# Placing the high and low parts of the activations in sixteen shifted tiles

## The chip, the core and the metric

The kernel runs on one core of a Trainium2 chip. The metric is the device time of one execution in microseconds (us). Three runs of the kernel before took 1261.02, 1261.59 and 1265.77 us; the median is 1261.59 us.

## What is computed

A decoder trunk of two layers on 512 tokens of width 1024, in float32. Cut to what matters here:

```python
for l in range(2):
    h = rmsnorm(x, attn_norm_w[l])
    proj = h @ w_in[l]                      # 22 tiles of 128 columns and one group of 148
    ...                                     # three mixers: state space, short convolution, sparse attention
    x = x + concat(y_ssd, y_sc, y_nsa) @ w_out[l]
    h = rmsnorm(x, ffn_norm_w[l])
    u = causal_dwconv(h @ ffn_w_up[l], ffn_conv_w[l], ffn_conv_b[l])   # 43 tiles of 128 columns
    gate, val = split(u)
    x = x + (silu(gate) * val) @ ffn_w_down[l]
return rmsnorm(x, final_norm_w)
```

## The kernel before

The activations lie transposed: eight tiles `x[k]` of 128 features by 512 tokens. A matmul that needs more precision than one float32r pass is made of three: each operand is split in a high part (rounded to float32r) and a low part (what the rounding left), and `mul3` (lines 185 to 190) multiplies weight high by activation high (L188), weight high by activation low (L189) and weight low by activation high (L190), all into one PSUM tile. The weights are the stationary operand, the activations are the moving one, 512 columns each time.

The activations of both norms are kept in `hs` (L90): eight tiles of 128 x 2 x 512, where `[:, 0, :]` is the high part and `[:, 1, :]` the low part, 2,048 bytes behind it in the same partition. `Norm.split` (L217 to 220) fills them: ScalarE writes the high part (L219), VectorE the low part (L220), 8 + 8 instructions for each of four norms. They are read

- by the 22 input-projection tiles of each layer (`tile_steps`, L430) and by the 43 up-projection tiles (`mtile`, L196), through `mul3`: 65 tiles x 8 values of k x 2 layers = 1,040 triples, 3,120 of the kernel's 5,843 matmuls;
- by `group_steps` (L450, L451), where a 128 x 128 piece of the activations is the stationary operand and the weights (148 columns, high and low) are the moving one: 64 matmuls with the high part and 64 with the low part. The weights' piece starts `(k % 4) * 148` elements into its tile.

All weights come in chunks of 128 x 1024 by DMA into `raw`; ScalarE and VectorE (or GpSimd) split them into `hl` (L163 to 166), three chunks ahead of their use. Products that are not of `hs` read their activations from `s` tiles (2,048 bytes each, a ring of 32) or from `yS`. `small` (L77) gives tiles of 256 bytes for columns and small matrices, from a ring of 21.

The order on every engine is that of the program: in the mixers one step of the projection stream (`pull`) is laid between pieces of the attention and of the state-space scan by a table of weights (`PLAN`); the feed-forward part is a plain sequence of tiles.

In the built program the tiles lie one behind the other in each partition, each start rounded up to a multiple of 32 bytes. `h0` starts at byte 32,928, that is 32 bytes behind a multiple of 64. As all that follows has sizes that are multiples of 64, every `h`, `hl`, `s` and `yS` tile starts 32 bytes behind a multiple of 64; `h` tiles start at 160 modulo 2,048, the other three at 672.

Of the kernel before, what the change touches and what calls it, by code (L numbers as in the profile page):

```python
# [10 lines left out]
F32 = mybir.dt.float32  # L11
F32R = mybir.dt.float32r
AF = mybir.ActivationFunctionType
OP = mybir.AluOpType
AX = mybir.AxisListType

P = 128
D = 1024
T = 512
NL = 2  # L20
KD = 8
# [4 lines left out]
NB = 148  # L26
# [37 lines left out]
def trunk(ctx: ExitStack, tc: tile.TileContext, ins, out):  # L64
    nc = tc.nc
    V, A, G, TE = nc.vector, nc.scalar, nc.gpsimd, nc.tensor

    per = ctx.enter_context(tc.tile_pool(name="per", bufs=1))
    pw = ctx.enter_context(tc.tile_pool(name="pw", bufs=3))
    ph = ctx.enter_context(tc.tile_pool(name="ph", bufs=1))  # L70
# [4 lines left out]
        return ph.tile(list(shape), dt, tag="s", bufs=32, name="s")  # L75

    def small(n, dt=F32):  # L77
        return ph.tile([P, 64], dt, tag="m", bufs=21, name="m")[:, :n]

    def mm():  # L80
        return pp.tile([P, 512], F32, tag="mm", bufs=3, name="mm")

    def aux():
        return pp.tile([P, 512], F32, tag="aux", bufs=4, name="aux")


    x = [per.tile([P, T], F32, name=f"x{k}") for k in range(KD)]
    mhalf = per.tile([P, 4], F32, name="mhalf")
    V.memset(mhalf, -0.5)
    hs = [per.tile([P, 2, T], F32R, name=f"h{k}") for k in range(KD)]  # L90
    par = [per.tile([P, NPAR], F32, name=f"par{l}") for l in range(NL)]
    cst = per.tile([P, K_COS], F32, name="cst")
    rot = per.tile([P, 2 * T], F32, name="rot")
# [75 lines left out]
    def nxt():  # L169
        i = st["use"]  # L170
        st["use"] += 1
        while st["dma"] < min(len(chunks), i + 5):
            do_dma(st["dma"])
            st["dma"] += 1
        while st["prep"] < min(len(chunks), i + 4):
            do_prep(st["prep"])
            st["prep"] += 1
        return hls.pop(i)
# [6 lines left out]
    def mul3(ps, wt, j, rhs_h, rhs_l, first, last):  # L185
        wh = wt[:, 0, j * P:(j + 1) * P]
        wl = wt[:, 1, j * P:(j + 1) * P]
        TE.matmul(ps, wh, rhs_h, start=first, stop=False)  # L188
        TE.matmul(ps, wh, rhs_l, start=False, stop=False)  # L189
        TE.matmul(ps, wl, rhs_h, start=False, stop=last)  # L190

    def mtile():
        wt = nxt()
        ps = mm()
        for k in range(KD):
            mul3(ps, wt, k, hs[k][:, 0, :], hs[k][:, 1, :], k == 0, k == KD - 1)  # L196
        return ps

    def col_rstd(dst, ps, n, width):
        v = small(n)  # L200
        V.tensor_scalar(v, ps, 1.0 / width, EPS, op0=OP.mult, op1=OP.add)  # L201
        G.tensor_tensor(dst, v, mhalf[:, :n], op=OP.pow)  # L202
# [4 lines left out]
    class Norm:  # L207
# [8 lines left out]

        def split(self, k):  # L217
            w = par[self.l][:, self.w + k:self.w + k + 1]
            A.activation(hs[k][:, 0, :], x[k], AF.Copy, scale=w)  # L219
            V.scalar_tensor_tensor(hs[k][:, 1, :], x[k], w, hs[k][:, 0, :].bitcast(F32), op0=OP.mult, op1=OP.subtract)  # L220

        def square(self, k, eng=V):
            sq = slot()
# [6 lines left out]
        def sums(self):  # L230
            ps = pp.tile([P, 512], F32, tag="pv", bufs=1, name="pv")
            acc = self.acc[V]
            if G in self.acc:
                V.tensor_tensor(acc, acc, self.acc[G], op=OP.add)
            for t in range(4):
                TE.matmul(ps[:, t:t + 1], acc[:, t * P:(t + 1) * P], ones[:, 0:1], start=True, stop=True)
            self.col = small(4)
            col_rstd(self.col, ps[:, 0:4], 4, D)
# [12 lines left out]
    def mixers(l, norm):  # L251
# [4 lines left out]
        def evac(ps, n):  # L256

            r, sw = slot(), slot()
            A.activation(r, ps, AF.Copy)
            for q in range(0, n, 64):  # L260
                A.activation(sw[q:q + 32], r[q + 32:q + 64], AF.Copy)
                A.activation(sw[q + 32:q + 64], r[q:q + 32], AF.Copy)
            return r, sw
# [68 lines left out]
        def post_b(t, ps):  # L332
            tmp = ph.tile([P, NB], F32, tag="btmp", bufs=2, name="btmp")
            c1 = cx["col"][:, t:t + 1]
            A.activation(tmp, ps[:, NB:2 * NB], AF.Copy, scale=c1)
            V.scalar_tensor_tensor(bV[:, t * P:(t + 1) * P], ps[:, 0:P], c1, tmp[:, 0:P], op0=OP.mult, op1=OP.add)
            V.scalar_tensor_tensor(bS[:, t, :], ps[:, P:NB], c1, tmp[:, P:NB], op0=OP.mult, op1=OP.add)
# [5 lines left out]
        def values():  # L343
            for b in range(2):
                v3 = Vv[b].rearrange("p (t c) -> p t c", c=P)
                s3 = bV.rearrange("p (t b d) -> p t b d", b=2, d=64)[:, :, b, :]
                A.activation(v3[:, :, 0:64], s3, AF.Copy)
                V.tensor_tensor(v3[:, :, 64:128], s3, v3[:, :, 0:64].bitcast(F32), op=OP.subtract)
            g3 = gate.rearrange("p (t c) -> p t c", c=12)
            A.activation(g3, bS[:, :, 8:20], AF.Tanh, scale=0.5)  # L350
            V.tensor_scalar(gate, gate, 0.5, 0.5, op0=OP.mult, op1=OP.add)
# [61 lines left out]
        def step():  # L413
            clock[0] += 1
            for e_ in [e_ for e_ in timed if e_[0] <= clock[0]]:
                timed.remove(e_)
                e_[1]()
            if clock[0] == t_sums:
                norm.sums()
                cx["col"] = norm.col  # L420
            if clock[0] == t_spread:
                first_norm()
                for p_ in late:
                    p_()

        def tile_steps(name, post, rot_n=0):
            wt = nxt()
            ps = mm()
            for k in range(KD):
                mul3(ps, wt, k, hs[k][:, 0, :], hs[k][:, 1, :], k == 0, k == KD - 1)  # L430
                step()
                if k < KD - 1:
                    yield
            args = evac(ps, rot_n) if rot_n else (ps,)
            if clock[0] < t_spread:
                late.append(lambda: post(*args))
            else:
                post(*args)
            done[name] = True
            yield  # L440

        def group_steps():
            pss = [aux() for _ in range(4)]
            for k in range(KD):
                if k % 4 == 0:
                    wt = nxt()
                w = wt[:, :, (k % 4) * NB:(k % 4 + 1) * NB]
                for t in range(4):
                    tok = slice(t * P, (t + 1) * P)
                    TE.matmul(pss[t][:, 0:2 * NB], hs[k][:, 0, tok], w, start=(k == 0), stop=False)  # L450
                    TE.matmul(pss[t][:, 0:NB], hs[k][:, 1, tok], w[:, 0, :], start=False, stop=(k == KD - 1))  # L451
                if k < KD - 1:
                    step()
                    yield
            late.append(lambda: [post_b(t, pss[t]) for t in range(4)] + [values()])
            step()
            done["group"] = True
            yield
# [59 lines left out]
        def cmp_mlp():  # L518
            pt = aux()
            for kv in range(2):  # L520
                for c in range(2):
                    o_ = TE.matmul(pt[:, kv * 32:kv * 32 + 32], hid[kv][:, c * P:(c + 1) * P], sel, start=(c == 0), stop=(c == 1))
                    if kv == 0 and c == 0:
                        pinned(0, o_)
            h_, t_ = small(64), small(64)
            A.activation(h_, pt[:, 0:64], AF.Copy)
            V.tensor_tensor(t_, h_, h_, op=OP.mult)
            V.tensor_scalar(t_, t_, 0.044715, 1.0, op0=OP.mult, op1=OP.add)
            V.tensor_tensor(t_, t_, h_, op=OP.mult)
            A.activation(t_, t_, AF.Tanh, scale=math.sqrt(2.0 / math.pi))  # L530
            V.scalar_tensor_tensor(h_, t_, 1.0, h_, op0=OP.add, op1=OP.mult)
            state["hid"] = h_
# [332 lines left out]
        for i, it in enumerate(items):  # L865
            t, b, k = it
# [40 lines left out]
        start, acc_w = pulled, 0  # L907
# [11 lines left out]
    def ffn(l, nf):  # L919
# [11 lines left out]
        def pair(i):  # L931
            if i == 0:
                ps = mtile()
                nf.sums()
                pv = mtile()
                nf.spread()
                g, v = up(0, ps), up(1, pv)
                A.activation(g, g, AF.Silu)
            else:
                g = up(2 * i, mtile())  # L940
                A.activation(g, g, AF.Silu)  # L941
                v = up(2 * i + 1, mtile())
            V.tensor_tensor(v, v, g, op=OP.mult)  # L943
            gh, gl = slot(F32R), slot(F32R)
            split(gh, gl, v)
            return gh, gl
# [100 lines left out]
    n = Norm(0, C_ANW)  # L1047
# [7 lines left out]
    for l in range(NL):  # L1055
        n = ffn(l, mixers(l, n))
# [105 lines left out]
```

## Time and profile before

| | us |
|---|---|
| median of 3 runs | 1261.59 |
| the profiled execution, its own time | 1265.31 |
| its span, first to last instruction | 1263.5 |
| TensorE (PE) busy in the span | 1208.4 |
| VectorE (DVE) busy | 879.8 |
| ScalarE (ACT) busy | 580.8 |
| GpSimd (POOL) busy | 221.8 |

The granted TensorE clock over the span was 0.981 of its full 2.4 GHz. The profiled execution took 3.7 us more than the median. A matmul's duration in the profile is from its start to its modelled end and overlaps the next; how long one occupies the engine is read from the distance between starts of neighbours, called pitch here.

### The profile page before, as it was taken

What the parts mean: (1) busy time and instruction counts of PE and PEld (TensorE: products, weight loads), DVE (VectorE), ACT (ScalarE), POOL (GpSimd) and SP (SyncE); (2) the same over time, 40 slices, a digit from 0 to 9 for tenths busy, and PEclk for the clock granted to TensorE, in tenths of its full rate; (3) what the DMA queues carried; (4) which work ended last, traced back from release to release, by engine and by line L of the source; (5) the groups of instructions that cost most, each with busy time, mean ns of one, the idle gap of its engine ahead of it and who ended that gap; (6) DMA issues with size and microseconds to landing.
All of it is one profiled execution on the core that took longest, in us unless ns stands there. A gap on an engine that the chain in (4) does not pass through costs nothing. (4 is left out here: it accounts for less than half of the span.)

```text
span 1263.5 us, 15487 instructions
## 1 busy us (share of the span) xinstructions
PE 1208.4 (96%) x5843; PEld 999.2 (79%) x5843; DVE 879.8 (70%) x1408; ACT 580.8 (46%) x909; POOL 221.8 (18%) x199
## 2 busy tenths in 40 slices
PE   8889899999999999999999888999999999999997
PEld 7667678788888888888877666778888888888897
DVE  6899979567776247776468998794587743677763
ACT  6655554354443124444347455434444422444553
POOL 3442337500000000000043332563000000000001
PEclk9989999999999999999999899999999999999999
DMA  7321123233223332332223211322233323333352
GB/s 259 113 67 51 51 84 101 67 100 98 88 98 100 100 99 90 95 117 87 84 84 100 67 51 51 103 98 83 84 100 101 100 88 96 100 100 100 122 165 99
DMA packets 37051, 121.33 MB, mean 96 GB/s; under 512 B 4144, under 2 KB 6512, under 8 KB 36976
## 3 DMA queue, kind: packets, MB, share of 16 engines
q1 hardware_dynamic: 36832, 120.33, 30.0%
q8 instruction: 46, 0.75, 0.3%
q14 instruction: 29, 0.24, 0.1%
q10 hardware_dynamic: 144, 0.00, 0.0%
HBM read 118.19 MB, written 2.13 MB: 95 GB/s over the span
## 5 line engine op out<-in xcount | busy, mean ns | idle before, releaser
L188 PE MATMUL mm<-h,hl 128*128 128x512 f32 x1040 | 413.6, 398 | 0.8 <-DVE s L359 0.8
L189 PE MATMUL mm<-h,hl 128*128 128x512 f32 x1040 | 410.3, 395 | 0.0
L190 PE MATMUL mm<-h,hl 128*128 128x512 f32 x1040 | 409.7, 394 | 0.0
L165 ACT ACTIVATE hl<-raw 128x1024 fp32r<-128x1024 f32 (+1 forms) x211 | 220.8, 1047 | 236.9 <-PE mm L190 129.5
L166 DVE TENSOR_TENSOR hl<-raw,hl 128x1024 fp32r<-128x1024 f32 (+1 forms) x167 | 203.4, 1219 | 110.3 <-ACT hl L165 108.1
L188 PEld LDWEIGHTS mm<-h,hl 128*128 128x128 f32 x1040 | 197.8, 190 | 42.0 <-issue 1.8
L190 PEld LDWEIGHTS mm<-h,hl 128*128 128x128 f32 x1040 | 197.4, 190 | 41.2 <-issue 0.2
L189 PEld LDWEIGHTS mm<-h,hl 128*128 128x128 f32 x1040 | 197.7, 190 | 39.6 <-issue 0.5
L202 POOL TENSOR_TENSOR m<-m,mhalf 128x1 f32<-128x1 f32 (+2 forms) x14 | 9.9, 709 | 773.7 <-DVE m L201 773.7
L166 POOL TENSOR_TENSOR hl<-raw,hl 128x1024 fp32r<-128x1024 f32 x44 | 108.3, 2464 | 150.5 <-ACT hl L165 144.8
L928 DVE SCALAR_TENSOR_TENSOR s<-s,par 128x511 f32<-128x511 f32 (+1 forms) x172 | 128.3, 748 | 3.5 <-ACT s L926 0.6
L925 DVE TENSOR_TENSOR s<-mm,rstdB 128x512 f32<-128x512 f32 x86 | 59.1, 689 | 66.1 <-PE mm L190 66.1
L189 PE MATMUL mm<-s,hl 128*128 128x512 f32 (+1 forms) x240 | 86.6, 361 | 3.4 <-DVE s L248 3.4
L188 PE MATMUL mm<-s,hl 128*128 128x512 f32 (+1 forms) x240 | 86.5, 360 | 1.1 <-ACT s L247 1.1
L190 PE MATMUL mm<-s,hl 128*128 128x512 f32 (+1 forms) x240 | 86.4, 360 | 0.0
L247 ACT ACTIVATE s<-s 128x512 fp32r<-128x512 f32 (+1 forms) x62 | 33.0, 545 | 111.8 <-DVE s L943 108.0
L188 PE MATMUL aux<-s,hl 128*128 128x512 f32 (+1 forms) x232 | 82.1, 354 | 0.0
L190 PE MATMUL aux<-s,hl 128*128 128x512 f32 (+1 forms) x232 | 81.8, 353 | 0.0
L189 PE MATMUL aux<-s,hl 128*128 128x512 f32 (+1 forms) x232 | 81.8, 353 | 0.0
L926 ACT ACTIVATE s<-s,par 128x512 f32<-128x512 f32 x86 | 69.2, 807 | 8.8 <-DVE s L925 8.1
L248 DVE TENSOR_TENSOR s<-s 128x512 fp32r<-128x512 f32 (+1 forms) x62 | 45.3, 741 | 27.9 <-ACT s L247 27.9
L941 ACT ACTIVATE s<-s 128x512 f32<-128x512 f32 x40 | 25.3, 632 | 79.0 <-DVE s L928 79.0
(252 smaller groups left out, 1648.9 us busy)
## 6 DMA issues: line engine op xcount, KB each, us to landing
raw<-in_w_up SPq DMA_DIRECT2D x86, 512.0 KB, 3.5
raw<-in_w_dn SPq DMA_DIRECT2D x54, 512.0 KB, 3.5
raw<-in_w_in SPq DMA_DIRECT2D x44, 512.0 KB, 3.5
raw<-in_w_out SPq DMA_DIRECT2D x16, 512.0 KB, 3.6
raw<-in_w SPq DMA_DIRECT2D x8, 512.0 KB, 3.6
s<-dr SPq DMA_DIRECT2D x16, 256.0 KB, 4.3
x<-in_xT SPq DMA_DIRECT2D x8, 256.0 KB, 5.8
out<-s SPq DMA_DIRECT2D x8, 256.0 KB, 3.4
```

Of the source, the lines that this page charges most:

```text
L165: A.activation(t[:, 0, a:b], r[:, a:b], AF.Copy)
L166: eng.tensor_tensor(t[:, 1, a:b], r[:, a:b], t[:, 0, a:b].bitcast(F32), op=OP.subtract)
L188: TE.matmul(ps, wh, rhs_h, start=first, stop=False)
L189: TE.matmul(ps, wh, rhs_l, start=False, stop=False)
L190: TE.matmul(ps, wl, rhs_h, start=False, stop=last)
L202: G.tensor_tensor(dst, v, mhalf[:, :n], op=OP.pow)
L247: A.activation(dst_h, src, AF.Copy)
L248: V.tensor_tensor(dst_l, src, dst_h.bitcast(F32), op=OP.subtract)
L925: V.tensor_tensor(u, ps, rstdB, op=OP.mult)
L926: A.activation(acc, u, AF.Identity, scale=w[:, 2:3], bias=pr[:, C_FCB + i:C_FCB + i + 1])
L928: V.scalar_tensor_tensor(acc[:, j:], u[:, :T - j], w[:, 2 - j:3 - j], acc[:, j:], op0=OP.mult, op1=OP.add)
L941: A.activation(g, g, AF.Silu)
```

## The change

The high and the low parts no longer share a tile. There are sixteen tiles of 528 elements (2,112 bytes, 33 times 64) in place of eight of 1,024. A high part is the first 512 elements of its tile. A low part starts 1, 2, 4, 8, 12, 6, 3 or 10 elements into its own, for k = 0 to 7: that is 4, 8, 16, 32, 48, 24, 12 and 40 bytes. The 1,024 bytes that this needs come from the ring of `small` tiles, 17 in place of 21.

In the built program `h0` still starts at byte 32,928, so all high parts still start 32 bytes behind a multiple of 64 (each next one 64 bytes further modulo 2,048). The low parts start 36, 40, 48, 0, 16, 56, 44 and 8 bytes behind a multiple of 64, for k = 0 to 7. Each `hl`, `s` and `yS` tile lies 1,024 bytes further on than before. On every engine the instructions, their order, and the semaphores and counts that each waits for are those of before; nothing but addresses differs.

```diff
     def small(n, dt=F32):
-        return ph.tile([P, 64], dt, tag="m", bufs=21, name="m")[:, :n]
+        return ph.tile([P, 64], dt, tag="m", bufs=17, name="m")[:, :n]
...
-    hs = [per.tile([P, 2, T], F32R, name=f"h{k}") for k in range(KD)]
+
+    hs = [per.tile([P, 528], F32R, name=f"h{k}")[:, 0:T] for k in range(KD)]
+    ls = [per.tile([P, 528], F32R, name=f"l{k}")[:, o:o + T] for k, o in enumerate((1, 2, 4, 8, 12, 6, 3, 10))]
...
-            mul3(ps, wt, k, hs[k][:, 0, :], hs[k][:, 1, :], k == 0, k == KD - 1)
+            mul3(ps, wt, k, hs[k], ls[k], k == 0, k == KD - 1)
...
-            A.activation(hs[k][:, 0, :], x[k], AF.Copy, scale=w)
-            V.scalar_tensor_tensor(hs[k][:, 1, :], x[k], w, hs[k][:, 0, :].bitcast(F32), op0=OP.mult, op1=OP.subtract)
+            A.activation(hs[k], x[k], AF.Copy, scale=w)
+            V.scalar_tensor_tensor(ls[k], x[k], w, hs[k].bitcast(F32), op0=OP.mult, op1=OP.subtract)
...
-                    TE.matmul(pss[t][:, 0:2 * NB], hs[k][:, 0, tok], w, start=(k == 0), stop=False)
-                    TE.matmul(pss[t][:, 0:NB], hs[k][:, 1, tok], w[:, 0, :], start=False, stop=(k == KD - 1))
+                    TE.matmul(pss[t][:, 0:2 * NB], hs[k][:, tok], w, start=(k == 0), stop=False)
+                    TE.matmul(pss[t][:, 0:NB], ls[k][:, tok], w[:, 0, :], start=False, stop=(k == KD - 1))
```

## Rows read from the trace of the kernel before

**Rows 1.** The page's first part: busy time, share of the span, instructions.

```profile
PE 1208.4 (96%) x5843; PEld 999.2 (79%) x5843; DVE 879.8 (70%) x1408; ACT 580.8 (46%) x909; POOL 221.8 (18%) x199
```

**Rows 2.** Windows: a feed-forward stretch, a mixer stretch, a stretch at half clock.

```profile
core 0: us, PE busy (x) PEld busy (x) DVE busy (x) ACT busy (x) POOL busy (x), PEclk, DMA share, GB/s
300.00:350.00 50.00, 50.00 (x222) 41.43 (x221) 38.13 (x49) 23.81 (x30) 0.00 (x0) 1.00 0.33 104
700.00:750.00 50.00, 42.75 (x202) 33.29 (x201) 45.84 (x87) 23.64 (x49) 15.64 (x11) 0.93 0.22 64
708.70:711.10 2.40, 2.40 (x7) 1.91 (x6) 2.05 (x9) 1.35 (x5) 0.00 (x0) 0.50 0.01 3
```

**Rows 3.** Groups of PE by shape; columns: count, busy us, mean ns, idle before.

```profile
line engine op names shapes xcount | busy us, mean ns | idle before us <-releasers
L188 PE MATMUL mm<-h,hl 128*128 128x512 f32 x1040 | 413.6, 398 | 0.8 <-DVE s L359 0.8
L189 PE MATMUL mm<-h,hl 128*128 128x512 f32 x1040 | 410.3, 395 | 0.0
L190 PE MATMUL mm<-h,hl 128*128 128x512 f32 x1040 | 409.7, 394 | 0.0
```

**Rows 4.** Timeline of PE, feed-forward: first and last of 25 neighbours; start, us.

```profile
330.13 0.39 PE L189 MATMUL mm<-h,hl 128*128 128x512 f32 x1
...
335.57 0.39 PE L189 MATMUL mm<-h,hl 128*128 128x512 f32 x1
```

**Rows 5.** Timeline of PE at half clock: first and last of 7 neighbours.

```profile
708.63 0.63 PE L188 MATMUL mm<-h,hl 128*128 128x512 f32 x1
...
711.19 0.46 PE L188 MATMUL mm<-h,hl 128*128 128x512 f32 x1
```

**Rows 6.** Timeline of PE, `s` tiles: 46 of 512 columns, 24 of 256.

```profile
399.72 0.39 PE L190 MATMUL mm<-s,hl 128*128 128x512 f32 x1
...
409.92 0.39 PE L190 MATMUL aux<-s,hl 128*128 128x512 f32 x1
...
1226.22 0.28 PE L189 MATMUL aux<-s,hl 128*128 128x256 f32 x1
...
1228.97 0.28 PE L188 MATMUL aux<-s,hl 128*128 128x256 f32 x1
```

**Rows 7.** Timeline of PE, group of layer 1: first matmul of k = 1 to 3, 5 to 7.

```profile
631.66 0.34 PE L450 MATMUL aux<-hl,h 128*128 128x296 f32 x1
...
632.65 0.34 PE L450 MATMUL aux<-hl,h 128*128 128x296 f32 x1
...
633.64 0.34 PE L450 MATMUL aux<-hl,h 128*128 128x296 f32 x1
...
636.51 0.34 PE L450 MATMUL aux<-hl,h 128*128 128x296 f32 x1
...
637.52 0.34 PE L450 MATMUL aux<-hl,h 128*128 128x296 f32 x1
...
638.52 0.34 PE L450 MATMUL aux<-hl,h 128*128 128x296 f32 x1
```

**Rows 8.** Groups of DVE by shape.

```profile
L928 DVE SCALAR_TENSOR_TENSOR s<-s,par 128x510 f32<-128x510 f32 x86 | 64.5, 750 | 3.0
L928 DVE SCALAR_TENSOR_TENSOR s<-s,par 128x511 f32<-128x511 f32 x86 | 64.1, 745 | 0.6 <-ACT s L926 0.6
...
L220 DVE SCALAR_TENSOR_TENSOR h<-x,par,h 128x512 fp32r<-128x512 f32 x32 | 23.7, 749 | 13.5 <-ACT h L219 13.3
```

**Rows 9.** Lines L451 and L537: weight loads, min/median/max ns, first and last start.

```profile
L451 PEld LDWEIGHTS aux<-hl,h x64: 186/192/333, 6.2 to 639.3; 128*128 128x128 f32 x64
...
L537 PEld LDWEIGHTS aux<-m,par x4: 187/188/259, 95.2 to 711.5; 128*128 128x128 f32 x4
```

More of the change, by code (lines that the diff above doesn't have):

```diff
@@ L429, in tile_steps @@
             for k in range(KD):
-                mul3(ps, wt, k, hs[k][:, 0, :], hs[k][:, 1, :], k == 0, k == KD - 1)
+                mul3(ps, wt, k, hs[k], ls[k], k == 0, k == KD - 1)
                 step()
```

## The prediction, made before the changed kernel ran

> **What bounds the kernel now.** I read the page's busy times first: TensorE is busy 1208.4 us of the span, VectorE, the next, 879.8 [rows 1]. Then the windows, stage by stage: in a feed-forward stretch TensorE is busy 50.00 of 50.00 us at full clock while VectorE and ScalarE have idle time; in a mixer stretch it still has 42.75 of 50.00, at a mean clock of 0.93 [rows 2]. So the end is set by how many matmuls there are and by the pitch of each. The groups show where they are: the 3 x 1040 that read `h` tiles [rows 3]. Their durations (394 to 398 ns) overlap and say little; the pitch comes from the timeline. Twenty-five neighbours in the feed-forward part start from 330.13 to 335.57 us [rows 4]: 5.44 / 24 = 226.7 ns. The columns alone take 512 / 2.4 GHz = 213.3 ns, so 13.3 ns a matmul remain, which I call the gap. At half clock seven neighbours start from 708.63 to 711.19 us [rows 5], granted clock 0.50 [rows 2]: 2.56 / 6 = 426.7 ns, which is 512 / 1.2 GHz with no gap. So whatever makes the gap runs beside the columns and is the slower of the two only at full clock. The gap is the same where the moving operand lies elsewhere: 46 neighbours that read `s` tiles start from 399.72 to 409.92, 10.20 / 45 = 226.7 ns; and with 256 columns, the second half of the tokens, where a read starts in the middle of its tile, 24 start from 1226.22 to 1228.97, 2.75 / 23 = 119.6 ns against 106.7 of columns, a gap of 12.9 [rows 6].
>
> **The change, part by part.** Order, waits and counts are unchanged on all five engines, so each part can cost only through an address.
>
> *High parts, 2,080 matmuls (L188, L190).* They start 32 bytes behind a multiple of 64 as before, only 64 bytes further from tile to tile. `h` tiles at 160 modulo 2,048 and `s` tiles at 672 have one pitch [rows 4, 6]. Cost 0. At best the gap would go: 2,080 x 13.3 ns = 27.7 us.
>
> *Low parts as moving operand, 1,040 matmuls (L189), 130 for each k.* These are on the path: nothing hides a longer pitch, neither in the feed-forward part nor in most of the mixers. Below, the whole gap goes: 1,040 x 13.3 = 13.9 us less. Above, a read at a bad start brings one column in the time that now brings two, as at half clock: 426.7 - 226.7 = 200 ns more, for all but k = 3 (whose low part now starts at a multiple of 64) 910 x 200 = 182 us. Between these ends the nearest row is the group: there the weights are the moving operand, and start 48, 0 and 16 bytes behind a multiple of 64 for k % 4 = 1, 2, 3, all multiples of 16. The eight matmuls of one k take 0.99 us (k = 1), 0.99 (k = 2), 1.01 (k = 5) and 1.00 (k = 6) [rows 7]: no difference between starts at 48 and at 0. One column where there were two would have added 4 x (296 + 148) / 2.4 = 740 ns to a k. These short matmuls are paced by other things too (the columns of one k need 740 ns of the 1,000), so a few ns could hide, but halved reading is excluded for such starts. That covers k = 2, 3 and 4. No row has TensorE stream an operand from a start that is no multiple of 16 (k = 0, 1, 5, 6, 7: 650 matmuls) or of 8 (k = 0, 6: 260). I take 0, since all that the rows do vary (32-byte shifts, place, length) leaves the pitch alone, and keep the ends for the range.
>
> [...]
>
> *Low parts as weights (L451, 64 loads).* L537's weights come from the parameter table, whose column 290 lies 8 bytes behind a multiple of 16. They load in 188 ns at the median, L451's in 192 [rows 9]. So 0 for six values of k; for the two odd starts, 16 loads, at most another load each: 16 x 0.19 = 3.1 us.
>
> *VectorE's writes of the low parts (L220, 32 instructions of 749 ns).* L928 is the same operation and writes 4 bytes into a tile with 511 columns and 8 bytes with 510: 745 and 750 ns [rows 8]. Cost 0; doubled, it would be 32 x 0.75 = 24 us of VectorE, and that row excludes it. [...]
>
> *Seventeen `small` tiles for 21, and all later tiles 1,024 bytes on.* No instruction gets a new wait or a higher count, so the shorter ring delays nothing; 1,024 is a multiple of 64, so nothing moves within a line. Cost 0.
>
> *Sum.* 1265.3 us for the profiled execution, +0. It is 3.7 us above the median of the runs, so 1261.6, which I give as **1262 us**. A measurement of this kernel tells about 0.5%, 6.3 us, from no change.
>
> **The rivals.**
>
> *An odd start halves the read (slower).* [...] Chance 0.08.
>
> *Every start off 16 bytes costs (slower).* If such a start repeats what makes the gap, 650 x 13.3 = +8.7 us, 1270; it decides from 9.7 ns each. Up to 21 ns each it stays under +14 us (1276). Chance 0.12 for this, 0.05 for much more (halved: 650 x 200 = 130 us, 1392). For it: the gap is a fixed cost per read, as a start would be. Against it: reads of 256 columns from the middle of a tile have the gap of reads of 512 from its head [rows 6].
>
> *The gap depends on place, and the shifts remove it (faster).* Every start of a moving read of 512 or 256 columns has so far been 32 bytes behind a multiple of 64, and tiles of one kind started at one place modulo 2,048, so the trace can't exclude that neighbours collide for that reason. Freed in the low parts alone: -13.9 us, 1248; in all 3,120: 3,120 x 13.3 = -41.6 us, 1220. For it: the shifts are new. Against it: neighbours at half a tile's distance, and `h` with `hl` at another distance than `s` with `hl`, show the same gap [rows 4, 6]. Chance 0.05 and 0.03.
>
> [...]
>
> That the change is undone by the layout can't be: the built program has the shifts.
>
> **How the numbers follow.** No effect beyond 0.5% has 0.67. Slower: 0.08 + 0.12 + 0.05 = 0.25. Faster: 0.05 + 0.03 = 0.08. The range goes from the low parts' whole gap (1261.6 - 13.9, rounded down to 1247) to 21 ns on each start off 16 bytes (1276); outside lie halved reads (0.13) and the gap gone everywhere (0.03), 0.16 in all. The forecast's own case is 1255 to 1268.
>
> **What would show it.** In the timeline of the changed kernel's feed-forward part: the pitch behind each L189. Right is 226.7 ns behind all eight low tiles and TensorE busy 50 of 50 us. Wrong is a pitch that differs by tile: by `l0` and `l6` alone (the first rival), by all five starts off 16 bytes (the second), or below 226.7 (the third). The low-part splits on VectorE should keep 749 ns, the group's eight matmuls 1.0 us a k, and no wait on a `small` tile should appear or grow.

## The result: 0.5 to 0.9% slower, from a longer pitch of the matmuls on `h` and `l` tiles

The changed kernel took 1270.43 us (median of 5 runs, 1268.78 to 1272.27), the kernel before 1263.78 us (5 runs, 1261.02 to 1265.77). The two medians divide to 1.005; the ratio on record is 1.007, 95% interval 1.005 to 1.009.

The profiled execution's span grew from 1263.5 to 1270.4 us. The page's first part and the groups of TensorE of the changed kernel answer to [rows 1] and [rows 3]; the instruction counts are the same, TensorE is busy 6.9 us longer, the others within 3.1 us of before.

```profile
PE 1215.3 (96%) x5843; PEld 996.6 (78%) x5843; DVE 880.1 (69%) x1408; ACT 577.7 (45%) x909; POOL 221.2 (17%) x199
...
L190 PE MATMUL mm<-h,hl 128*128 128x512 f32 x1040 | 415.0, 399 | 0.8 <-DVE s L361 0.8
L192 PE MATMUL mm<-h,hl 128*128 128x512 f32 x1040 | 413.0, 397 | 0.1
L191 PE MATMUL mm<-l,hl 128*128 128x512 f32 x1040 | 412.1, 396 | 0.0
```

The durations hardly tell (1 to 3 ns), the pitch does. In the timeline of TensorE (start in us, duration) two whole tiles of the up-projection, 48 pitches, lie between these rows of the changed kernel:

```profile
315.70 0.39 PE L190 MATMUL mm<-h,hl 128*128 128x512 f32 x1
...
326.81 0.39 PE L190 MATMUL mm<-h,hl 128*128 128x512 f32 x1
```

That is 11.11 / 48 = 231.5 ns where [rows 4] had 226.7. It is not one number any more: read at the trace's nanosecond, averaged over the settled feed-forward tiles (the third of a layer and the next ones) and place by place, the 24 pitches of a tile lie between 224.2 and 241.7 ns. Behind high parts (L190, L192) the mean is 231.5 ns, behind low parts (L191) 231.2. The sum over a tile is 5553 ns against 5440 before, 113 ns more (the expectation of e1_lines below writes 5446 for before; the settled tiles have 5440). Undisturbed pitches of matmuls that read `s` and `yS` tiles stayed at 226.7.

Where the time went, by stages: starts of the first feed-forward matmul and of layer 1's group, in the timeline of TensorE of before,

```profile
276.80 0.39 PE L188 MATMUL mm<-h,hl 128*128 128x512 f32 x1
...
630.41 0.30 PE L450 MATMUL aux<-hl,h 128*128 128x296 f32 x1
...
895.12 0.39 PE L188 MATMUL mm<-h,hl 128*128 128x512 f32 x1
```

and of the changed kernel:

```profile
275.52 0.39 PE L190 MATMUL mm<-h,hl 128*128 128x512 f32 x1
...
633.94 0.30 PE L452 MATMUL aux<-hl,h 128*128 128x296 f32 x1
...
897.07 0.39 PE L190 MATMUL mm<-h,hl 128*128 128x512 f32 x1
```

The feed-forward part of layer 0 went from 353.6 to 358.4 us (+4.8), what follows 895.12 or 897.07 to the end of the span from 368.4 to 373.3 (+4.9). 43 tiles by 113 ns are 4.9 us, so the pitch accounts for both. The two mixer stages became 1.3 and 1.6 us shorter, though their 22 tiles have the longer pitch too wherever they run back to back. The windows of the two stages, of before and of the changed kernel (columns as in [rows 2]):

```profile
0.00:275.00 275.00, 250.37 (x1217) 201.09 (x1218) 221.50 (x425) 146.65 (x275) 110.56 (x98) 0.96 0.30 99
...
630.00:905.00 275.00, 253.37 (x1266) 204.50 (x1265) 213.61 (x416) 141.39 (x263) 104.57 (x92) 0.97 0.26 80
```

```profile
0.00:275.00 275.00, 249.47 (x1222) 199.08 (x1223) 222.35 (x426) 147.96 (x277) 110.02 (x98) 0.98 0.31 100
...
630.00:905.00 275.00, 254.32 (x1273) 205.18 (x1272) 214.46 (x417) 141.34 (x263) 104.55 (x92) 0.98 0.26 81
```

TensorE waits there for other engines in part of the time (it is busy 250 of 275 us), and it was granted 0.98 of its clock in place of 0.96 and 0.97. What the clock is worth is seen in two kernels of the next section, e9_plain and e10_line. Both have the pitch of before, and the feed-forward part of layer 0 takes 353.6 us in both, at a granted clock of 1.00. One execution of each was profiled. The first feed-forward matmul in the timeline of TensorE, and the first window (columns as in [rows 2]), of e9_plain:

```profile
277.31 0.39 PE L190 MATMUL mm<-h,hl 128*128 128x512 f32 x1
...
0.00:275.00 275.00, 251.10 (x1214) 200.90 (x1215) 220.74 (x425) 146.69 (x275) 110.61 (x98) 0.95 0.31 99
```

and of e10_line:

```profile
275.30 0.39 PE L189 MATMUL mm<-h,hl 128*128 128x512 f32 x1
...
0.00:275.00 275.00, 248.53 (x1223) 200.62 (x1224) 222.40 (x427) 147.86 (x277) 110.11 (x98) 0.97 0.31 100
```

The mixer stage took 2.0 us less at 0.97 than at 0.95. e1_lines, which has the long pitch, was granted 0.97 there too and starts its first feed-forward matmul at 276.73 us, 1.4 us behind e10_line; its second mixer stage took 262.2 us at 0.99, that of e10_line 261.0 at 0.98. So the longer pitch does cost time in the mixers, and the higher clock of this one profiled execution hid it. The same holds for the whole: six executions of the kernel before with a granted clock of 0.986 over the span (in the comparisons below) have spans of 1258.1 to 1261.6 us, mean 1259.8; the two of the changed kernel with 0.986 have 1270.4 and 1270.5. At equal clock the loss is some 10.6 us, 0.8%; the 6.9 us between the two profiles are less because the profile of before was granted 0.981. That the change itself raised the clock is not shown: e1_lines and e2_bytes, with the same loss of pitch, were granted 0.984 to 0.989.

### The profile page after: what moved, and what is told of

Same layout as the page of the kernel before. It is cut to its first block, busy times and chain, and to the rows that moved or that the text cites. A ratio compares the mean times of both kernels' runs of the same rounds, so it can differ in the third digit from the quotient of the medians.

```text
span 1270.4 us, 15487 instructions
## 1 busy us (share of the span) xinstructions
PE 1215.3 (96%) x5843; PEld 996.6 (78%) x5843; DVE 880.1 (69%) x1408; ACT 577.7 (45%) x909; POOL 221.2 (17%) x199
## 5 line engine op out<-in xcount | busy, mean ns | idle before, releaser
L190 PE MATMUL mm<-h,hl 128*128 128x512 f32 x1040 | 415.0, 399 | 0.8 <-DVE s L361 0.8
L192 PE MATMUL mm<-h,hl 128*128 128x512 f32 x1040 | 413.0, 397 | 0.1
L191 PE MATMUL mm<-l,hl 128*128 128x512 f32 x1040 | 412.1, 396 | 0.0
L190 PEld LDWEIGHTS mm<-h,hl 128*128 128x128 f32 x1040 | 197.3, 190 | 44.8 <-issue 1.8
L192 PEld LDWEIGHTS mm<-h,hl 128*128 128x128 f32 x1040 | 196.8, 189 | 43.9 <-DVE hl L168 0.5
L191 PEld LDWEIGHTS mm<-l,hl 128*128 128x128 f32 x1040 | 196.9, 189 | 43.6 <-issue 0.5
L191 PE MATMUL mm<-s,hl 128*128 128x512 f32 (+1 forms) x240 | 86.6, 361 | 3.4 <-DVE s L250 3.4
L190 PE MATMUL mm<-s,hl 128*128 128x512 f32 (+1 forms) x240 | 86.5, 361 | 0.8 <-ACT s L249 0.8
L192 PE MATMUL mm<-s,hl 128*128 128x512 f32 (+1 forms) x240 | 86.4, 360 | 0.0
L190 PE MATMUL aux<-s,hl 128*128 128x512 f32 (+1 forms) x232 | 82.1, 354 | 0.0
L192 PE MATMUL aux<-s,hl 128*128 128x512 f32 (+1 forms) x232 | 81.9, 353 | 0.0
L191 PE MATMUL aux<-s,hl 128*128 128x512 f32 (+1 forms) x232 | 81.8, 353 | 0.0
```

## The experiments

Three theories stood after the result. **A1**: the pitch depends on the distance, modulo some power of two, between the moving operand that is streamed and the weights that are loaded beside it (in the changed kernel PEld is busy 996.6 us and PE 1215.3 of a span of 1270.4, so the two overlap). **A2**: it depends on the distance between one moving operand and the next. **B**: it depends on where inside a line a read starts, as the second rival of the prediction had it. A line stands here for 64 bytes, the step by which tiles were moved. All kernels below compute the whole. Where tiles need more room, the ring of `small` tiles gives it, which the code shown leaves out: 19 tiles in e2_bytes and e4_w0123, 18 in e5_w4567, 15 in e6_wbytes to e8_w200to252, 20 in e10_line. `...` marks lines left out.

**e1_lines: only the shift by lines.** Of the changed kernel:

```diff
-    ls = [per.tile([P, 528], F32R, name=f"l{k}")[:, o:o + T] for k, o in enumerate((1, 2, 4, 8, 12, 6, 3, 10))]
+    ls = [per.tile([P, 528], F32R, name=f"l{k}")[:, 0:T] for k in range(KD)]
```

> Edit: the sixteen tiles of 33 lines stay, but the low parts start at the head of theirs, so every start is again 32 bytes behind a multiple of 64 and only the shift by whole lines of 64 bytes is left. In the changed kernel's feed-forward part the pitch is no longer one number: the 24 matmuls of a tile take 5554 ns where they took 5446, single pitches between 225 and 240 ns. Theory A (the shift by lines, against the weights or between neighbours, makes the pitch): the mean pitch of matmuls on h and l tiles stays near 231 ns and the ratio to before near 1.007. Theory B (the starts inside a line make it, as the second rival had it): the pitch is back at 226.7 ns everywhere and the ratio is 1.000.

Measured: 1273.21 us, ratio 1.0093 (1.0070 to 1.0115). The timeline of e1_lines over one tile of 24:

```profile
317.02 0.39 PE L190 MATMUL mm<-h,hl 128*128 128x512 f32 x1
...
322.58 0.39 PE L190 MATMUL mm<-h,hl 128*128 128x512 f32 x1
```

5.56 / 24 = 231.7 ns. Starts inside a line are not needed for the loss: shifts by whole lines make all of it. Theory B as the only cause falls. The settled pitches repeat within the tile: those of k = 4 to 7 are those of k = 0 to 3 within 0.2 ns (225.7, 236.0, 228.3 ns for k = 0 and for k = 4), a first sign of a period of four lines.

**e2_bytes: only the starts inside a line.** Of the changed kernel:

```diff
...
-    hs = [per.tile([P, 528], F32R, name=f"h{k}")[:, 0:T] for k in range(KD)]
-    ls = [per.tile([P, 528], F32R, name=f"l{k}")[:, o:o + T] for k, o in enumerate((1, 2, 4, 8, 12, 6, 3, 10))]
+    hs = [per.tile([P, T], F32R, name=f"h{k}") for k in range(KD)]
+    low = per.tile([P, KD * T + 128], F32R, name="low")
+    ls = [low[:, k * T + o:(k + 1) * T + o] for k, o in enumerate((1, 2, 3, 4, 6, 8, 10, 12))]
```

> Edit: high parts in eight tiles of 2,048 bytes and low parts behind each other in one tile, starting 4, 8, 12, 16, 24, 32, 40 and 48 bytes further than a multiple of 2,048 would have them, so no shift by whole lines is left and only the starts inside a line. Theory A: pitch 226.7 ns for all 24 matmuls of a tile, ratio 1.000. Theory B: the mean pitch is near 231 ns with the low parts' pitches the long ones, ratio near 1.007; if only odd starts cost, the low parts of k = 0 and 2 alone are longer; if starts off 16 bytes, those of k = 0, 1, 2, 4 and 6.

Measured: 1273.58 us, ratio 1.0095 (1.0076 to 1.0115). One tile of 24 in the timeline of e2_bytes:

```profile
314.65 0.40 PE L191 MATMUL mm<-h,hl 128*128 128x512 f32 x1
...
320.22 0.40 PE L191 MATMUL mm<-h,hl 128*128 128x512 f32 x1
```

5.57 / 24 = 232.1 ns. So shifts of some bytes alone make the loss too, and here also the pitches behind high parts, which had not moved, are between 224 and 241 ns. Starts off 16 bytes do not stand out: behind the five low parts that have them the mean is 233.2 ns, behind the other three 234.1. Each of the two halves of the change is enough, which neither A with whole lines alone nor B had expected; a distance counted in bytes would give it.

**e3_pairs: pairs of k at one place.** Of the changed kernel:

```diff
-    hs = [per.tile([P, 528], F32R, name=f"h{k}")[:, 0:T] for k in range(KD)]
-    ls = [per.tile([P, 528], F32R, name=f"l{k}")[:, o:o + T] for k, o in enumerate((1, 2, 4, 8, 12, 6, 3, 10))]
+    SIZES = (512, 528, 512, 528, 512, 528, 512, 592)
+    hs = [per.tile([P, n], F32R, name=f"h{k}")[:, 0:T] for k, n in enumerate(SIZES)]
+    ls = [per.tile([P, n], F32R, name=f"l{k}")[:, 0:T] for k, n in enumerate(SIZES)]
```

> Edit: low parts at the head of their tiles, and high and low parts of k = 0 and 1 shifted by no line against the weights, of 2 and 3 by one line of 64 bytes, of 4 and 5 by two, of 6 and 7 by three. Within a pair neighbours lie at the same place modulo 512, so only the distance to the weights differs by pair. Theory A1 (the distance of the moving operand to the weights being loaded beside it sets the pitch): k = 0 and 1 at 226.7 ns, the other pairs each at a pitch of their own, away from 226.7. Theory A2 (the distance between two neighbouring moving operands sets it): 226.7 ns inside every pair, another pitch only at the steps from one pair to the next (k = 1 to 2, 3 to 4, 5 to 6, 7 to 0). Theory B: 226.7 ns everywhere.

Measured (one run): 1273.96 us. In the pair of k = 6 and 7 the pitch settled, in the timeline of e3_pairs

```profile
321.39 0.39 PE L191 MATMUL mm<-h,hl 128*128 128x512 f32 x1
...
322.56 0.39 PE L193 MATMUL mm<-h,hl 128*128 128x512 f32 x1
```

1.17 / 5 = 234 ns (233.3 averaged over the settled feed-forward tiles, within 0.1 ns at every place). Neighbours of this pair lie at the same place modulo 512, so A2 has no reason for it. But k = 0 and 1 were not at 226.7 as A1 had it: they go 226, 236, 228, 233, 231, 227 ns. The pitch had not come to rest within these six, so six matmuls at one distance can show too little. The next kernels give each distance 24.

**e4_w0123, e5_w4567, e6_wbytes: the weights moved, the activations not.** Of the kernel before; the four buffers of split weights become four tiles with padding behind them, or with an offset `o` ahead of the data, and are used in turn:

```diff
...
-        t = pw.tile([P, 2, 1024], F32R, tag="hl", bufs=4, name="hl")
+        n = st["hl"] % 4
+        st["hl"] += 1
+        full = pw.tile([P, (2064, 2064, 2064, 2128)[n]], F32R, tag=f"hl{n}", bufs=1, name=f"hl{n}")
+        t = full[:, 0:2048].rearrange("p (e n) -> p e n", e=2)
```

e5_w4567 has tiles of 2064 and 256 bytes of padding ahead of `par`; e6_wbytes has tiles of 2176 and `full[:, o:o + 2048]` with o = 1, 2, 4, 8. (The scheduler put a few matmuls of the mixers in another order; the readings are from the feed-forward part.)

> Edit, of the kernel before: activations as before, but the four buffers of the split weights (hl) start 0, 1, 2 and 3 lines of 64 bytes further than a multiple of 512 from the h tiles. Each tile of 24 matmuls takes its weights from one buffer, in turn, so each stretch of 24 has one distance between what streams and what is loaded, and no distance between neighbouring streams changes. Theory A1 (that distance sets the pitch): four pitches by turns, 226.7 ns for the first buffer and 233.3 for the fourth (e3_pairs settled at 233.3 where the distance was three lines), the other two between 225 and 240. Theory A2 (the distance between neighbouring streams sets it): 226.7 ns throughout. Theory B (starts inside a line): 226.7 ns throughout.

> Edit, of the kernel before: as e4_w0123, with 4, 5, 6 and 7 lines. Theory A1: four pitches by turns, none of them 226.7 ns unless the pattern repeats within 512 bytes; if some distance is better than the one of the kernel before, its 24 matmuls take less than 24 x 226.7 = 5440 ns. Theories A2 and B: 226.7 ns throughout.

> Edit, of the kernel before: the four buffers of the split weights start 4, 8, 16 and 32 bytes further than a multiple of 512 from the h tiles. Theory A1, with the distance counted in bytes: four pitches by turns, away from 226.7 ns. With the distance counted in whole lines of 64 bytes: 226.7 ns for all four, and then what e2_bytes showed comes from the place of the moving read itself. Theory A2 with bytes: 226.7 ns throughout.

Measured (one run each): 1275.65, 1271.88 and 1272.17 us, the kernel before 1260.59. Four tiles that follow each other in the timeline of e4_w0123, from the seventh matmul to the last, 17 pitches each:

```profile
323.90 0.39 PE L191 MATMUL mm<-h,hl 128*128 128x512 f32 x1
...
327.76 0.39 PE L193 MATMUL mm<-h,hl 128*128 128x512 f32 x1
...
329.38 0.40 PE L191 MATMUL mm<-h,hl 128*128 128x512 f32 x1
...
333.35 0.39 PE L193 MATMUL mm<-h,hl 128*128 128x512 f32 x1
...
334.98 0.39 PE L191 MATMUL mm<-h,hl 128*128 128x512 f32 x1
...
338.92 0.39 PE L193 MATMUL mm<-h,hl 128*128 128x512 f32 x1
...
340.54 0.39 PE L191 MATMUL mm<-h,hl 128*128 128x512 f32 x1
...
344.43 0.40 PE L193 MATMUL mm<-h,hl 128*128 128x512 f32 x1
```

3.86, 3.97, 3.94 and 3.89 us by 17: 227.1, 233.5, 231.8 and 228.8 ns for 0, 1, 2 and 3 lines, four pitches by turns as A1 said. The expectation had 233.3 ns for the fourth buffer, and the second has it: e3_pairs had moved the activations by three lines, which puts the weights one line behind them modulo four, so the distance has a sign, which the expectation had wrong. No activation moved and no distance between neighbouring streams inside a tile is new, so A2 is not what does it here. The second tile of e5_w4567, with five lines, has

```profile
325.67 0.40 PE L192 MATMUL mm<-h,hl 128*128 128x512 f32 x1
...
329.64 0.39 PE L194 MATMUL mm<-h,hl 128*128 128x512 f32 x1
```

again 3.97 / 17 = 233.5 ns; its four means (226.7, 233.5, 232.2, 228.9) are those of e4_w0123 one by one. So the pattern repeats every four lines, 256 bytes. Bytes count too: e6_wbytes has means of 232.3, 230.8, 232.7 and 233.4 ns for 4, 8, 16 and 32 bytes.

The mean at 16 bytes hides two values. From the seventh matmul to the last, 17 pitches each, the first tile of the long stretch (it follows four matmuls of 128 columns on other tiles), and the next tile from the same buffer, in the timeline of e6_wbytes:

```profile
286.35 0.39 PE L192 MATMUL mm<-h,hl 128*128 128x512 f32 x1
...
290.20 0.40 PE L194 MATMUL mm<-h,hl 128*128 128x512 f32 x1
...
308.54 0.40 PE L192 MATMUL mm<-h,hl 128*128 128x512 f32 x1
...
312.50 0.39 PE L194 MATMUL mm<-h,hl 128*128 128x512 f32 x1
```

3.85 / 17 = 226.5 ns and 3.96 / 17 = 232.9 ns (226.6 and 233.3 at the trace's nanosecond). In each layer that first tile has the pitch of distance 0 and the nine others 233.3 to 233.4. So the distance alone does not fix the pitch: at 16 bytes the two tiles behind those four matmuls have another than the rest.

**e9_plain: the change without its shifts.** Of the changed kernel:

```diff
-    hs = [per.tile([P, 528], F32R, name=f"h{k}")[:, 0:T] for k in range(KD)]
-    ls = [per.tile([P, 528], F32R, name=f"l{k}")[:, o:o + T] for k, o in enumerate((1, 2, 4, 8, 12, 6, 3, 10))]
+    hs = [per.tile([P, T], F32R, name=f"h{k}") for k in range(KD)]
+    ls = [per.tile([P, T], F32R, name=f"l{k}") for k in range(KD)]
+    per.tile([P, 256], F32, name="gap")
```

> Edit, of the changed kernel: all that it changes but the shifts. Sixteen separate tiles, a ring of 17 small tiles, all later tiles 1,024 bytes on, but every high and low part starts at a multiple of 256 bytes from the weights, as before. Theory A1 (the pitch goes by the distance modulo 256 bytes between the streamed operand and the weights loaded beside it): 226.7 ns for every matmul on h and l tiles, ratio 1.000, no part of the changed kernel's loss left. Its rival, that separate tiles, the shorter ring or the move of the later tiles hold part of the loss: a ratio between 1.002 and 1.007, with a pitch of 226.7 ns or not.

Measured: 1262.32 us (12 runs), ratio 0.9995 (0.9979 to 1.0010). One tile of 24 in its timeline:

```profile
316.81 0.39 PE L190 MATMUL mm<-h,hl 128*128 128x512 f32 x1
...
322.25 0.39 PE L190 MATMUL mm<-h,hl 128*128 128x512 f32 x1
```

5.44 / 24 = 226.7 ns. Separate tiles, the ring of 17 and the move of all later tiles cost nothing that can be measured. Within the interval, the shifts are the whole loss.

**e7_w96to240 and e8_w200to252: is there a better distance?** As e6_wbytes, with o = 24, 40, 56, 60 and o = 50, 54, 62, 63.

> Edit, of the kernel before: the four buffers of the split weights start 96, 160, 224 and 240 bytes further than a multiple of 256 from the h tiles. Distances 0, 4, 8, 16, 32, 64, 128 and 192 gave mean pitches of 226.7, 232.3, 230.8, 232.7, 233.4, 233.5, 232.2 and 228.9 ns. Theory A1: four more, each settled in a cycle of its own between 226 and 236 ns. Open is whether 0 is the best distance: one below 226.7 ns would give a kernel faster than before, some 4,300 matmuls of 512 columns by the difference; none does if the distance 0 is where streams and loads never meet.

> Edit, of the kernel before: as e7_w96to240, with 200, 216, 248 and 252 bytes. Theory A1: four more settled pitches between 226 and 236 ns; 252, four bytes short of the distance 0, tells whether one element off is as bad on this side as on the other (4 bytes: 232.3 ns). Below 226.7 ns only if 0 is not the best distance.

Measured (one run each): 1279.51 and 1265.52 us. From the third and the fourth buffer (248 and 252 bytes) in the timeline of e8_w200to252:

```profile
330.47 0.40 PE L192 MATMUL mm<-h,hl 128*128 128x512 f32 x1
...
334.44 0.39 PE L194 MATMUL mm<-h,hl 128*128 128x512 f32 x1
...
336.03 0.39 PE L192 MATMUL mm<-h,hl 128*128 128x512 f32 x1
...
339.88 0.39 PE L194 MATMUL mm<-h,hl 128*128 128x512 f32 x1
```

3.97 / 17 = 233.5 and 3.85 / 17 = 226.5 ns. All sixteen distances tried, with the mean pitch from the seventh matmul of a tile on, over the feed-forward tiles of that buffer:

| weights behind the moving operand, bytes modulo 256 | mean pitch, ns |
|---|---|
| 0, 240, 252 | 226.7, 226.8, 226.7 |
| 4, 8, 16, 32 | 232.3, 230.8, 232.7, 233.4 |
| 64, 96, 128, 160 | 233.5, 234.1, 232.2, 233.4 |
| 192, 200, 216, 224, 248 | 228.9, 230.6, 231.8, 233.3, 233.4 |

At 16 bytes 18 tiles have 233.4 and 2 have 226.7; at 128 bytes 18 have 232.0 and 2 have 233.6. No mean is below 226.7. The expectation that 240 and 252 would have pitches of their own was a miss, and the pattern is not smooth: 252 is as good as 0, 248 as bad as most. The kernel before sits at the best value found, so these runs point to no version faster than both.

**e10_line: all starts at a multiple of 64.** Of the kernel before:

```diff
+    per.tile([P, 8], F32, name="gap")
     hs = [per.tile([P, 2, T], F32R, name=f"h{k}") for k in range(KD)]
```

> Edit, of the kernel before: 32 bytes of padding ahead of the h tiles, so that all h, hl, s and yS tiles start at a multiple of 64 bytes instead of 32 behind one; no distance between streams and weights changes. Theory A1 (only the distance modulo 256 counts): 226.7 ns everywhere and a ratio of 1.000. Its rival, the third one of the prediction in a narrower form (the 13.3 ns beyond the columns come in part from where in a line of 64 bytes a read starts): a shorter pitch, by up to 13.3 ns for some 4,300 matmuls of 512 columns, a ratio between 0.955 and 0.995.

Measured: 1261.91 us (12 runs), ratio 1.0006 (0.9988 to 1.0024). One tile of 24 in its timeline:

```profile
314.80 0.39 PE L189 MATMUL mm<-h,hl 128*128 128x512 f32 x1
...
320.24 0.39 PE L189 MATMUL mm<-h,hl 128*128 128x512 f32 x1
```

226.7 ns, with all these tiles at a multiple of 64 as with all of them 32 bytes behind one. Between these two places the common start makes no difference, and the gap of 13.3 ns is the same at both. This also rules out that the weights' own place alone sets the pitch: moved by 32 bytes alone they gave 233.4 ns (e6_wbytes), moved by 32 bytes together with the activations 226.7.

## Why the prediction was wrong in its forecast, point by point

The time lies in the range, and the forecast case, no change within 0.5% (1255 to 1268 us), did not come. The interval of the ratio (0.5 to 0.9%) lies on the slower side. That the range holds the time is luck: its upper end, 1276 us, was reckoned for reads that start off 16 bytes, and that is not what happened.

- **What bounds the kernel**: right. TensorE's pitch in the feed-forward part carried the loss (+9.7 us there; the span grew by 6.9 only, because the profiled execution was granted more clock in the mixers).
- **High parts, 2,080 matmuls, cost 0**: this step failed. It read [rows 4] and [rows 6] as "place does not matter", because `h` at 160 and `s` at 672 modulo 2,048 have one pitch. But `h`, `s`, `yS` and `hl` all lay multiples of 256 bytes apart, and 256 is the period (e4_w0123 against e5_w4567). The rows had varied the place only in steps that can't be seen. High parts, moved by 64 bytes a tile against the weights, lengthened too: with shifts by lines alone the mean pitch is 230.6 ns behind high parts and 233.8 behind low ones (e1_lines), against 226.7.
- **Low parts as moving operand, 0**: wrong with the same cause. The nearest row taken, the group [rows 7], does vary the distance between what streams and what is loaded (the weights start 592 bytes further with each k, which leaves 80, 160 and 240 modulo 256 for `k % 4` = 1, 2 and 3), but among matmuls of 148 and 296 columns, eight of which take 0.99 to 1.01 us [rows 7] where their columns need some 0.74 (an estimate at twice the rate of [rows 5]); a difference of 5 ns in 226.7 could not be read there, as the prediction itself said of a few ns.
- **Weights of L451, VectorE's writes, the ring of 17, the later tiles**: no loss shows there. e9_plain covers the last two (0.9995). In the changed kernel the weight loads of L453 (L451 before) take 192 ns at the median, as before, and VectorE's writes of the low parts 750 ns, 749 before.
- **The first rival** (odd starts read half as fast): did not happen. No run shows a halved read, the term behind its 0.08 and behind the 0.13 outside the range: 426.7 ns was measured at a granted clock of 0.50 alone [rows 5], and at full clock no settled pitch of the changed kernel's feed-forward part is above 241.7.
- **The second rival** (every start off 16 bytes costs): its 1270 us is the time measured, by coincidence. Its mechanism is not what happened: e1_lines has no such start and lost 0.9%, and in e2_bytes the low parts off 16 bytes are no longer than the others (233.2 and 234.1 ns).
- **The third rival** (the pitch depends on place) named the right cause, that all places so far were alike modulo a power of two, and had the wrong sign: the distance that the kernel before has is the best of those tried. It also looked at neighbouring streams and at `h` with `hl`, and took the latter as told by the rows.
- **The sum**: the two terms put at 0 measured, by 3,120 matmuls and 231.4 - 226.7 = 4.7 ns, +14.7 us if all are paced by TensorE. The 2,064 in the feed-forward part showed in full (+9.7). Those in the mixers showed in part at most: 1.4 us in the first mixer stage, e1_lines against e10_line at a granted clock of 0.97, where 22 tiles by 113 ns would be 2.5.

## What to carry to other kernels

Before a layout is called harmless because places differ already, look at the differences modulo small powers of two: tiles whose sizes are all multiples of 512 vary nothing below that. In this kernel, with one weight load for each matmul (5843 of both [rows 1]), the weights are best kept a multiple of 256 bytes from the moving operands: padding either side by a line of 64 bytes or by some bytes cost 2 to 7 ns in 227 for all the distances tried but 240 and 252 bytes. And before two profiles of one execution each are set against each other, compare their granted clocks: 0.981 against 0.986 hid a third of this loss. A layout can be scanned cheaply by giving each of a ring of buffers another offset and reading the pitch by turns.

## What the runs showed of the hardware

- The pitch of matmuls with 512 columns changes when only the weights' place changes: 226.7 ns at a distance of 0, 233.5 at 64 bytes, with a period of 256 bytes (e4_w0123, e5_w4567). Moving weights and activations together by 32 bytes changes nothing (226.7, e10_line). Only the distance between these two was moved: the runs show that the pitch goes with it, and leave open what makes it do so, and whether the weights' load or another access to the same tile is what counts.
- After a change of distance the pitch settles into a repeating pattern: in e4_w0123 at 64 bytes 230.8 and 235.8 ns by turns, at 192 bytes 231.7, 225.8 and 229.2, at 0 a constant. The distance does not fix the pattern alone: at 64 bytes e3_pairs has a constant 233.3, and at 16 bytes e6_wbytes has 226.7 in 2 tiles and 233.4 in 18. Where the distance changes at every step, as in the changed kernel, no single pitch comes; the 24 pitches repeat from tile to tile.
- At a granted clock of 0.50, 512 columns take 426.7 ns [rows 5], so 213.3 at twice the rate, which is the prediction's 512 / 2.4 GHz; at full clock 256 columns more take 226.7 - 119.6 = 107.1 ns [rows 4, 6], 2.39 a ns. The 13.3 ns that the pitch at full clock has beyond 213.3 are there, or more, in the mean at every distance tried and at both common starts (e8_w200to252, e10_line). What makes them stays open.
